# An RWKV mixer with a compact state, its token shift and masks partly on ScalarE, and another order of the trunk

## The chip, the cores and the metric

The kernel runs on one core of a Trainium2 chip. The core has a matrix engine (TensorE, PE in the profile, with its weight loads shown apart as PEld), VectorE (DVE), ScalarE (ACT), GpSimd (POOL) and SyncE (SP), which issues the transfers. TensorE writes to PSUM, eight banks of 128 partitions by 512 float32; the other data lie in SBUF. The metric is the device time of one execution in microseconds.

## The reference

Two layers over 256 tokens of width 1024. In each layer there is a SwiGLU feed-forward with a layer norm, a mixer whose output goes with a cross attention over 256 memory tokens through `w_out` into a second layer norm, and a second feed-forward with a third:

```python
x = layer_norm(ALPHA * x + 0.5 * swiglu(x, ffn1_w_gate[i], ffn1_w_up[i], ffn1_w_down[i]), ...)
proj = x @ w_in
heads = concat([mixer(proj[..., :k]), memory_attention(proj[..., k:], mem_k, mem_v)])
x = layer_norm(ALPHA * x + heads @ w_out[i], ...)
x = layer_norm(ALPHA * x + 0.5 * swiglu(x, ffn2_w_gate[i], ffn2_w_up[i], ffn2_w_down[i]), ...)
```

Layer 0 mixes by RWKV-7 with 12 heads of 64, layer 1 by stick-breaking attention. What the RWKV mixer computes:

```python
z = p + (prev - p) * mu                         # token shift, prev is the token before
kk = k * k_k; kk = kk * rsqrt(max(sum(kk * kk), 1e-24))
sa = state @ kk_t                               # for each token t, head by head, state 64x64
state = state * w_t - outer(sa, kk_t * a_t) + outer(v_t, k_t)
out_t = state @ r_t
```

and behind it a norm over each head, a bonus of r, k and v, and a gate.

## The kernel before, in words

**Tiling.** The 256 tokens are two halves of 128, each on the 128 partitions. A feed-forward of 2816 is cut into 11 blocks of 256 columns. For a block the gate and up weights come in four pieces of 128x1024 float32 and the down weights in two. `piece` splits each into a rounded part `hi` (a copy on ScalarE) and a rest `lo` (a subtraction on VectorE), and `mm3` makes one product out of three float32r matmuls (hi by hi, hi by lo, lo by hi). A block in the list `WHOLE` takes its down weights unsplit, as a plain float32 matmul, which the hardware does in two passes that the trace shows as two entries.

**Blocks for one half or for both.** A block is either *shared* (loaded once, used by both halves) or *solo* (loaded for one half alone, and again for the other). `LAGS` says how many blocks are solo. While a half is in its mixer, the other half's solo blocks are run beside it: `alternate` takes steps of the mixer and of the blocks in turns, by a table of weights (`RW` for RWKV, `SB` for the stick mixer), `HOLD` and `TAIL` say how many solo blocks are kept back for the time of `w_out` and for the end.

**The order.** Nothing is issued when it is written. `Plan` records every operation with its reads and writes, and a list scheduler with built-in durations puts them on the engines; it repeats this 24 times with shaken priorities from a fixed seed and keeps the shortest plan. The buffers (10 raw, 9 hi and 9 lo weight pieces; two PSUM banks for each of the tags `tp`, `gu`, `acc0`, `acc1`) are given out by the same plan. So each edit of the program or of a number can move instructions everywhere, and every instruction that is planned bears one line of the kernel (L606 before, L602 after, in `issue`); the names of the tiles tell them apart. A name ending in r with a number is a buffer, not a variable: `ps_2r` and `ps_3r` are the `tp` banks, `ps_26r` and `ps_27r` the `gu` banks, `ps_22r` to `ps_25r` the two `acc` pairs, and one buffer can hold several tiles in turn.

**The RWKV mixer** (`rwkv`) runs once per half, in two chunks of 64 tokens. `shifted` projects up to 512 columns, turns them (transposes into a `tp` bank), copies the turned part to SBUF, subtracts neighbouring tokens on VectorE and adds `mu` times the difference. Keys are normalised: two tensors (`qr[:, :, 0]` and `bt`) are each multiplied by the inverse norm. A triangular system of 64x64 per head and chunk is solved in blocks of 16, and doubled twice with masked copies of `L` (`_LEVELS`). Then the chunks follow one another: the state `S` takes 128 partitions (two heads of 64 in a pair) by 6 pairs by 2 by 64, with a pair's two 64x64 blocks on the diagonal of a 128x128 square and zeros off it. The output part from the state is

```python
nc.tensor.matmul(Ov[j // 3][cs, 2 * (j % 3):2 * (j % 3) + 2].rearrange("q h d -> q (h d)"), qr[:, j, 1, cs],
                 S[:, j].rearrange("p a d -> p (a d)"), start=False, stop=False)
```

and the state is updated in four parts of 64 rows, each by an addition from PSUM and a product with the decay.

**The gate of a feed-forward block** is either Tanh on ScalarE with two products on VectorE, or Silu with one. Before, `beside` chose by the stage: Tanh in the blocks beside a mixer, Silu elsewhere.

Of the kernel before, what the change touches and what calls it, by code (L numbers as in the profile page):

```python
# [21 lines left out]
P = 128  # L22
# [24 lines left out]
LAGS = ((5, 8), (4, 8))  # L47
FIRST = 2
PRE = (0, 0)
RW = dict(p0=0, p1=0, p2=0, p3=0, p4=0.5, lb=0, sub=14, rb=0.5, kq=1, nat=10, dy=4, dt=1.5, c0=1.0, c1=1, c2=6, c3=2, t0=0, t1=10)  # L50
SB = dict(z0=3.0, z1=0, ln=2.0, e0=1.0, e1=1.5, o=12)
HOLD = (2, 4)
TAIL = (2, 2)
# [5 lines left out]
BESIDE = (True, False)  # L59
WHOLE = (((0, 1, 2, 3, 4, 5, 6, 8, 9, 10), (0, 1, 2, 4, 5, 6, 7, 9)), ((3,), ()))  # L60
# [9 lines left out]
_LEVELS = [16, 32]  # L70


def _constants():
    i = np.arange(P)
    c, s = i // C, i % C
    t = np.arange(C)
    cols = {}
    cols["ident"] = np.eye(P)
    tri = np.zeros((P, 2, C + 1))
    for cc in range(2):  # L80
        tri[:, cc, :] = (c[:, None] == cc) & (s[:, None] <= np.arange(C + 1)[None, :] - 1)
    cols["tric"] = (-math.exp(-0.5) * tri).reshape(P, -1)
    mqr = np.stack([t[None, :] > s[:, None], t[None, :] >= s[:, None]], 1)
    cols["mqr"] = mqr.reshape(P, -1)
    lv = []
    for b in _LEVELS:
        lv.append((s[:, None] // (2 * b) == t[None, :] // (2 * b)) & (s[:, None] // b % 2 == 1) & (t[None, :] // b % 2 == 0))
    cols["lvl"] = np.stack(lv, 1).reshape(P, -1)
# [49 lines left out]
class Plan:  # L138
# [11 lines left out]
    @contextmanager  # L150
    def together(self):

        self.bundle = []
        yield
        o, self.bundle = self.bundle[0], None
        self.close(o)
# [453 lines left out]
def kernel(ctx, tc, const, x, mem, f1g, f1u, f1d, f2g, f2u, f2d, ln_g, ln_b, w_out, w_mem_kv,  # L610
# [22 lines left out]
    lvl = K_("lvl").rearrange("p (l t) -> p l t", t=C)  # L633
# [317 lines left out]
    def rwkv_constants():  # L951
# [6 lines left out]
        vc = cp.tile([P, 44], F32, tag="vc", name="vc")  # L958
        pt = ps("tp")
        nc.tensor.transpose(pt[:, :44], vrow, ident[:44, :44])  # L960
        nc.copy(vc, pt[:, :44])
        for n, a, b in (("mu", 0, 20), ("a0", 20, 26), ("k_k", 26, 32), ("k_a", 32, 38), ("r_k", 38, 44)):
# [3 lines left out]
        S = new(cp, [P, NT, 2, HD], F32, "S", "S")  # L966
# [5 lines left out]
    def rwkv(hf, res):  # L972
        ac = f"acc{hf}"
        mu, a0, k_k, k_a = R["mu"], R["a0"], R["k_k"], R["k_a"]
# [6 lines left out]
        def shifted(c0, n, dest):  # L981

            pn = project(hf, rw_in[0], c0, n)
            nt = min(n, SHIFT - c0) // P
            ch0 = c0 // P
            ptv = turned(pn, 0, n // P)
            pT = new(tp_, [P, 4, P + 1], F32, "tb", "pT", 2)
            came = nc.copy(pT[:, :nt, 1:], ptv[:, :nt])
            nc.vector.tensor_copy(pT[:, :nt, 0], lastc[:, ch0:ch0 + nt]).after.append(came.i)
            if hf < NHALF - 1:  # L990
                nc.vector.tensor_copy(lastc[:, ch0:ch0 + nt], pT[:, :nt, P])
            d = pn.rearrange("p (i t) -> p i t", t=P)
# [3 lines left out]
            if nt < n // P:  # L996
                mq = new(mp, [P, 2, P], F32, "mq", "mq")
                nc.copy(mq, ptv[:, nt:n // P], 0.125)
                return mq


        zl = sl("zl", [P, 2, P])
        mq = shifted(2304, 512, lambda i: zl[:, i])
# [46 lines left out]
        shifted(768, 512, lambda i: zk[:, i])  # L1050
        shifted(1280, 512, lambda i: zk[:, 4 + i] if i < 2 else zv[:, i - 2])
# [10 lines left out]
        nc.vector.tensor_mul(cv4(qr[:, :, 0]), cv4(bt), e1[:, :, :, 0:C])  # L1062
        nc.vector.tensor_mul(bt, bt, a)
# [20 lines left out]
        shifted(0, 512, lambda i: zr[:, i])  # L1084
        shifted(512, 256, lambda i: zr[:, 4 + i])
# [10 lines left out]
        shifted(1792, 512, lambda i: zv[:, 2 + i])  # L1096
# [125 lines left out]
        for l in range(len(_LEVELS)):  # L1222
            lastl = l == len(_LEVELS) - 1
            Lm, Y = hv(sl("Lm")), hv(sl("Y"))
            nc.vector.tensor_tensor(Lm, L, bc(lvl[:, l], 1, [P, NH, C]), ALU.mult)
# [49 lines left out]
        with nc.together():  # L1275
            for i in range(NH):
                for cs in both:
                    nc.tensor.matmul(Ov[i // 6][cs, i % 6], Sk[cs, i, 1], V[cs, i], start=i % 6 == 0, stop=False)
        yield "c0"
        for c, cs in enumerate(both):  # L1280
            first = hf == 0 and c == 0
            if not first:
                xs = six("tp")
                with nc.together():
                    for j in range(NT):
                        for p in range(2):
                            pr = slice(p * HD, (p + 1) * HD)
                            nc.tensor.matmul(xs[p][cs, j], qr[pr, j, 0, cs], S[pr, j, p], start=True, stop=True)
# [4 lines left out]
            with nc.together():  # L1293
                for i in range(NH):
                    nc.tensor.matmul(ub[i // 6][cs, i % 6], Tt[cs, i], X[cs, i], start=True, stop=True)
                    if c == 1:
                        nc.tensor.matmul(Ov[i // 6][both[0], i % 6], RB[both[0], i], U[both[0], i], start=False, stop=i % 6 == 5)
            nc.copy(U[cs, 0:6], ub[0][cs], -1.0)
            nc.copy(U[cs, 6:12], ub[1][cs], -1.0)
            if not first:  # L1300
                with nc.together():
                    for j in range(NT):
                        nc.tensor.matmul(Ov[j // 3][cs, 2 * (j % 3):2 * (j % 3) + 2].rearrange("q h d -> q (h d)"), qr[:, j, 1, cs],
                                         S[:, j].rearrange("p a d -> p (a d)"), start=False, stop=False)
            yield "c2"
            if not (hf == NHALF - 1 and c == 1):
                for g in range(2):
                    sb = ps("tp")
                    for a, b in ((kn, V), (bn, U)):
                        with nc.together():  # L1310
                            for i in range(6):
                                pr = slice(i % 2 * HD, (i % 2 + 1) * HD)
                                h = 6 * g + i
                                nc.tensor.matmul(sb[pr, i // 2 * HD:(i // 2 + 1) * HD], a[cs, h * HD:(h + 1) * HD], b[cs, h],
                                                 start=a is kn and i < 2, stop=a is bn and i >= 4)
                    for p in range(2):
                        pr = slice(p * HD, (p + 1) * HD)
                        st = S[pr, 3 * g:3 * g + 3, p]
                        nc.vector.tensor_tensor(st, st, sb[pr, :3 * HD].rearrange("q (i d) -> q i d", i=3), ALU.add)
                        nc.vector.tensor_tensor(st, st, bc(pc[pr, 3 * g:3 * g + 3, c], 2, [HD, 3, HD]), ALU.mult)  # L1320
                    yield "c3"
        with nc.together():
            for i in range(NH):
                nc.tensor.matmul(Ov[i // 6][both[1], i % 6], RB[both[1], i], U[both[1], i], start=False, stop=i % 6 == 5)
# [3 lines left out]
        for g in range(2):  # L1328
            gs = slice(6 * g, 6 * g + 6)
            nc.scalar.activation(sqo[:, gs], Ov[g], AF.Square)  # L1330
            nc.vector.tensor_tensor(o[:, gs], Ov[g], lg[:, gs], ALU.mult)
            nc.vector.tensor_reduce(hs[:, 0, gs], sqo[:, gs], AX.X, ALU.add)
# [147 lines left out]
    def blocks(w, seq, beside=False, whole=()):  # L1480
        waiting = []
        for c, halves in seq:
            hidden = yield from ffn_block(w, c, halves, beside, c in whole)
# [8 lines left out]
    for i in range(DEPTH):  # L1492
# [19 lines left out]
        run(blocks(w, solo(1, range(HEAD)), BESIDE[0], WHOLE[i][0]))  # L1512
        alternate(chain_steps(mixer(0, mixed)), blocks(w, solo(1, range(HEAD, lag1)), True, WHOLE[i][0]), steps)
# [11 lines left out]
        alternate(second, blocks(w, solo(0, range(lag2 - HOLD[i])), True, WHOLE[i][1]), steps)  # L1525
        run(chain_steps(mixed_out(1, mixed[1], w_out[i])), blocks(w, solo(0, range(lag2 - HOLD[i], lag2)), BESIDE[1], WHOLE[i][1]))
# [31 lines left out]
```

## Time and profile before

| | |
|---|---|
| median of the runs | 1084.11 us (1083.97 to 1085.16, 3 runs) |
| profiled execution | 1085.55 us, its span 1083.5 us |
| TensorE busy, matmul entries | 1063.7 us (98%), 6213 |
| VectorE busy, instructions | 890.6 us (82%), 1267 |
| ScalarE busy, instructions | 721.0 us (67%), 990 |
| bytes moved | 300.14 MB, mean 277 GB/s |
| granted TensorE clock | 0.997 of full |

A row of a window gives the stretch, its length, the busy time of PE, PEld, DVE, ACT and POOL with the count of instructions, then the granted clock, the mean share of the 16 DMA engines and GB/s. A row of a tile gives the operation, its count, the shortest, median and longest duration in ns, first and last start, and the shapes. A row of a timeline gives start, duration, operation, count. A wait gives who waited for whom, the sum in us, how often, and the longest. Ends of matmuls are modelled and overlap; the distance between two starts is what a matmul takes of the queue.

### The profile page before, as it was taken

To read this page: it belongs to the slowest core of one execution; us is meant where nothing else is said; L and a number is where in the kernel's file an instruction comes from. 1 tells how busy PE (TensorE), PEld (TensorE's weight loads), DVE (VectorE), ACT (ScalarE), POOL (GpSimd) and SP (SyncE) were. 2 spreads that over 40 slices of the span, in tenths; PEclk is the share of its full clock that TensorE was granted. 3 is DMA by queue.
4 is the path that set the end of the run, shared out by engine and by line. 5 is a ranking of instruction groups with operands and counts; after the bars stand their busy time and mean duration, and the time that the engine had idled before them with its cause. 6 is when DMAs were issued, how large, how long until landed. Compare 5 with 4: busy or idle time off the path is not lost.

```text
span 1083.5 us, 17483 instructions
## 1 busy us (share of the span) xinstructions
PE 1063.7 (98%) x6213; PEld 848.4 (78%) x6213; DVE 890.6 (82%) x1267; ACT 721.0 (67%) x990; POOL 2.7 (0%) x14
## 2 busy tenths in 40 slices
PE   7999999999999999999999999999999999999996
PEld 5888887867788777778888888888877787888885
DVE  6676679997999998787779965559889979987777
ACT  6565568765588774656658545547996999776652
POOL 0000000000000000000000000000000000000000
PEclk9999999999999999999999999999999999999998
DMA  9997869477797797699889976758978987999881
GB/s 312 335 355 243 261 211 363 134 256 250 216 317 262 237 312 259 221 344 317 261 264 353 335 252 197 225 182 274 372 275 283 389 310 236 394 368 304 258 284 58
DMA packets 210073, 300.14 MB, mean 277 GB/s; under 512 B 13716, under 2 KB 157248, under 8 KB 209986
## 3 DMA queue, kind: packets, MB, share of 16 engines
q1 hardware_dynamic: 209986, 299.03, 81.7%
q8 instruction: 48, 0.79, 0.3%
q14 instruction: 39, 0.32, 0.1%
HBM read 297.93 MB, written 1.05 MB: 276 GB/s over the span
## 4 chain that ended last, share of the span: by engine, by line
PE 94%; DVE 4%; DMA 1%; ACT 0%; issue 0%; SPq 0%; DVEq 0%; ACTq 0%
PE ps_27r L606 27%; PE ps_26r L606 27%; PE ps_25r L606 8%; PE ps_24r L606 8%; PE ps_22r L606 8%; PE ps_23r L606 8%; PE ps_3r L606 4%; PE ps_2r L606 4%; DMA raw_42r<-in_ffn_w_down_dram 1%; DVE x L606 1%; DMA raw_6r<-in_ffn_w_up_dram 0%; DVE Y_337r L606 0%; DVE xTl L606 0%; SPq L606 0%; DVE lo_5r L606 0%
## 5 line engine op out<-in xcount | busy, mean ns | idle before, releaser
L606 PE MATMUL ps_26r<-hi_4r,xTh 128*128 128x512 f32 x54 | 22.5, 416 | 2.8 <-ACT hi_4r L606 2.8
L606 ACT ACTIVATE h_32r<-ps_26r 128x256 f32<-128x256 f32 (+1 forms) x29 | 12.4, 426 | 18.9 <-PE ps_26r L606 18.9
L606 PE MATMUL ps_27r<-hi_19r,xTh 128*128 128x512 f32 x56 | 23.7, 423 | 0.0
L606 ACT ACTIVATE h_31r<-ps_27r 128x256 f32<-128x256 f32 (+1 forms) x32 | 13.5, 423 | 14.2 <-PE ps_27r L606 12.6
L606 PE MATMUL ps_27r<-hi_43r,xTh 128*128 128x512 f32 x54 | 22.2, 411 | 0.0
L606 PE MATMUL ps_26r<-lo_5r,xTh 128*128 128x512 f32 x54 | 21.7, 402 | 0.5 <-DVE lo_5r L606 0.5
L606 PE MATMUL ps_27r<-hi_7r,xTh 128*128 128x512 f32 x54 | 22.1, 410 | 0.0
L606 PE MATMUL ps_27r<-hi_16r,xTh 128*128 128x512 f32 x52 | 22.1, 425 | 0.0
L606 PE MATMUL ps_27r<-hi_19r,xTl 128*128 128x512 f32 x56 | 21.9, 391 | 0.0
L606 PE MATMUL ps_27r<-lo_20r,xTh 128*128 128x512 f32 x56 | 21.9, 391 | 0.0
L606 PE MATMUL ps_27r<-hi_4r,xTh 128*128 128x512 f32 x54 | 21.7, 402 | 0.0
L606 PE MATMUL ps_26r<-hi_4r,xTl 128*128 128x512 f32 x54 | 21.6, 400 | 0.0
L606 PE MATMUL ps_27r<-lo_44r,xTh 128*128 128x512 f32 x54 | 21.2, 393 | 0.2 <-DVE lo_44r L606 0.2
L606 PE MATMUL ps_26r<-hi_40r,xTh 128*128 128x512 f32 (+1 forms) x54 | 21.2, 393 | 0.0
L606 PE MATMUL ps_27r<-hi_43r,xTl 128*128 128x512 f32 x54 | 21.1, 392 | 0.0
L606 PE MATMUL ps_27r<-lo_8r,xTh 128*128 128x512 f32 x54 | 21.1, 391 | 0.0
L606 PE MATMUL ps_27r<-hi_7r,xTl 128*128 128x512 f32 x54 | 21.1, 391 | 0.0
L606 PE MATMUL ps_27r<-lo_5r,xTh 128*128 128x512 f32 x54 | 21.1, 391 | 0.0
L606 PE MATMUL ps_27r<-hi_4r,xTl 128*128 128x512 f32 x54 | 21.1, 390 | 0.0
L606 ACT ACTIVATE h_32r<-ps_27r 128x256 f32<-128x256 f32 (+1 forms) x25 | 10.6, 425 | 15.7 <-PE ps_27r L606 15.5
L606 PE MATMUL ps_26r<-hi_16r,xTh 128*128 128x512 f32 x52 | 21.0, 403 | 0.0
L606 PE MATMUL ps_26r<-hi_37r,xTh 128*128 128x512 f32 (+1 forms) x52 | 20.9, 402 | 0.0
(1918 smaller groups left out, 3951.5 us busy)
## 6 DMA issues: line engine op xcount, KB each, us to landing
raw_45r<-in_ffn_w_down_dram SPq DMA_DIRECT2D x18, 512.0 KB, 5.9
raw_18r<-in_ffn_w_gate_dram SPq DMA_DIRECT2D x33, 256.0 KB, 4.6
raw_18r<-in_ffn_w_up_dram SPq DMA_DIRECT2D x33, 256.0 KB, 3.0
raw_21r<-in_ffn_w_gate_dram SPq DMA_DIRECT2D x32, 256.0 KB, 4.3
raw_21r<-in_ffn_w_up_dram SPq DMA_DIRECT2D x32, 256.0 KB, 5.4
raw_15r<-in_ffn_w_down_dram SPq DMA_DIRECT2D x16, 512.0 KB, 5.3
raw_42r<-in_ffn_w_down_dram SPq DMA_DIRECT2D x15, 512.0 KB, 5.0
raw_15r<-in_ffn_w_gate_dram SPq DMA_DIRECT2D x29, 256.0 KB, 5.4
```

Of the source, the lines that this page charges most:

```text
L606: fn(*[at(x) for x in a], **{n: at(x) for n, x in k.items()})
```

## The change

- **State.** `S` loses its zero half: 128 partitions by 6 pairs by 64. The output part from the state is made head by head, with 64x64 matmuls like those of the product beside it; the output banks `Ov` hold the even and the odd heads instead of the lower and the upper six. The update of a chunk uses one PSUM bank and one addition and one product over all partitions. New orders between some of these steps are fixed by `after`.
- **Token shift.** The turned part isn't copied: ScalarE writes it times 1 - mu (`omm`), 128 columns at a time, and VectorE adds mu times the neighbour, read from PSUM. The last column of a group is kept by ScalarE or VectorE; for half 1 a small product `ml` and an addition bring in the column before.
- **Masks.** The masked copies of `L` are made by ScalarE with a mask on the partitions (`odd`, `quad`), on a tile that GpSimd clears.
- **Keys.** Only `bt` is multiplied by the inverse norm, and `qr[:, :, 0]` is made from it.
- **Gating.** `TANH` lists the blocks with Tanh, for each layer and feed-forward. Beside the mixer of half 1 in layer 0, block 4 becomes Silu, in layer 1 block 3.
- **Order.** `RW`, `SB`, `HOLD`, `TAIL`, `WHOLE` change; in layer 1's second feed-forward nine blocks are solo instead of eight.

The core of the diff:

```diff
-LAGS = ((5, 8), (4, 8))
+LAGS = ((5, 8), (4, 9))
-RW = dict(..., c0=1.0, c1=1, c2=6, c3=2, t0=0, t1=10)
-SB = dict(z0=3.0, z1=0, ln=2.0, e0=1.0, e1=1.5, o=12)
-HOLD = (2, 4)
-TAIL = (2, 2)
+RW = dict(..., c0=8, c1=3, c2=6, c3=2, t0=0, t1=1.5)
+SB = dict(z0=0, z1=0, ln=2.0, e0=1.0, e1=1.5, o=12)
+HOLD = (2, 3)
+TAIL = (3, 3)
-BESIDE = (True, False)
-WHOLE = (((0, 1, 2, 3, 4, 5, 6, 8, 9, 10), (0, 1, 2, 4, 5, 6, 7, 9)), ((3,), ()))
+TANH = (((0, 1, 2, 3, 4), (0, 1, 2, 3, 5, 9)), ((0, 1, 2, 3, 9), (0, 1, 2)))
+WHOLE = (((1, 2, 3, 4, 5, 6, 8, 9), (0, 1, 2, 4, 5, 6, 7, 9)), ((3,), ()))
...
-            came = nc.copy(pT[:, :nt, 1:], ptv[:, :nt])
-            nc.vector.tensor_copy(pT[:, :nt, 0], lastc[:, ch0:ch0 + nt]).after.append(came.i)
...
-            nc.vector.tensor_sub(d[:, :nt], pT[:, :nt, 0:P], pT[:, :nt, 1:])
-            for i in range(nt):
-                nc.vector.scalar_tensor_tensor(dest(i), d[:, i], mu[:, ch0 + i:ch0 + i + 1], pT[:, i, 1:], ALU.mult, ALU.add)
+                for q in range(m):
+                    nc.scalar.activation(dest[:, q], ptv[:, i + q], AF.Copy, scale=omm[:, ch + q:ch + q + 1])
+                    nc.vector.scalar_tensor_tensor(dest[:, q, 1:], ptv[:, i + q, :P - 1], mu[:, ch + q:ch + q + 1], dest[:, q, 1:], ALU.mult, ALU.add)
+                if hf > 0:
+                    nc.vector.tensor_tensor(dest[:, :, 0], dest[:, :, 0], ml[:, ch:ch + m], ALU.add)
...
-            for dst in (qr[:, :, 0, cs], bt[:, :, cs]):
-                nc.vector.tensor_mul(dst, dst, b_[c])
+            nc.vector.tensor_mul(bt[:, :, cs], bt[:, :, cs], b_[c])
+        nc.vector.tensor_mul(cv4(qr[:, :, 0]), cv4(bt), e1[:, :, :, 0:C])
...
-            nc.vector.tensor_tensor(Lm, L, bc(lvl[:, l], 1, [P, NH, C]), ALU.mult)
+                    nc.copy(Lm[:, :, ts], L[:, :, ts], K_("odd")[:, q:q + 1])
+                nc.copy(Lm[:, :, :2 * BLK], L[:, :, :2 * BLK], quad[:, 1:2])
...
+                    for j in range(NT):
+                        for p in range(2):
+                            pr = slice(p * HD, (p + 1) * HD)
+                            nc.tensor.matmul(Ov[p][cs, j], qr[pr, j, 1, cs], S[pr, j], start=j == 0 and c == 0, stop=False)
...
+                nc.vector.tensor_tensor(S, S, sb, ALU.add)
+                nc.vector.tensor_tensor(S, S, bc(pc[:, :, c], 2, [P, NT, HD]), ALU.mult)
```

What the plan makes of it, at three places. On TensorE, layer 0, half 0, between the first and the second chunk: `vn` by `kn` and `Lm` by `bn` are the state update, `S` by `qr` the products with the state, `hi` and `lo` the memory keys' projection beside them. Before, from the update to the product into the output banks `ps_22r` and `ps_23r`:

```order
L606 MATMUL ps_3r<-vn_307r,kn_306r 64x64 x6
L606 MATMUL ps_3r<-Lm_327r,bn_383r 64x64 x6
L606 MATMUL ps_2r<-vn_307r,kn_306r 64x64 x6
L606 MATMUL ps_2r<-Lm_327r,bn_383r 64x64 x6
L606 MATMUL ps_27r<-hi_43r,hi_7r 128x512
...
L606 MATMUL ps_3r<-S_110r,qr_376r 64x64
L606 MATMUL ps_2r<-S_110r,qr_376r 64x64
...
L606 MATMUL ps_22r<-S_110r,qr_376r 64x128 x3
L606 MATMUL ps_23r<-S_110r,qr_376r 64x128 x3
```

and after:

```order
L602 MATMUL ps_2r<-vn_311r,kn_310r 64x64 x12
L602 MATMUL ps_2r<-Lm_330r,bn_384r 64x64 x12
L602 MATMUL ps_25r<-raw_18r,hT_486r 128x512
L602 MATMUL ps_26r<-hi_43r,hi_13r 128x512
...
L602 MATMUL ps_23r<-S_110r,qr_377r 64x64
L602 MATMUL ps_22r<-S_110r,qr_377r 64x64
...
L602 MATMUL ps_3r<-S_110r,qr_377r 64x64
L602 MATMUL ps_2r<-S_110r,qr_377r 64x64
```

The update is one group in one bank, the product into the output banks comes first and in the same small form, and less other work stands between the update and the products that read the state.

On ScalarE, layer 0, half 0, in the projections of the mixer: `hi` is a weight split, `h` a copy of a projection, `pT` the turned part, `L` the shifted keys, `RB` and `g` the gates. Before:

```order
L606 ACTIVATE hi_16r<-raw_42r 128x1024
L606 ACTIVATE h_31r<-ps_26r 128x512
L606 ACTIVATE hi_43r<-raw_15r 128x1024
L606 ACTIVATE g_333r<-ps_22r 128x384
L606 ACTIVATE pT_324r<-ps_2r 128x4x128
L606 ACTIVATE g_333r<-ps_23r 128x384
```

and after:

```order
L602 ACTIVATE lastc<-ps_2r 128x4
L602 ACTIVATE RB_333r<-ps_23r,vc 128x128
L602 ACTIVATE L_345r<-ps_2r,vc 128x128
L602 ACTIVATE hi_19r<-raw_39r 128x1024
L602 ACTIVATE hi_16r<-raw_15r 128x1024
L602 ACTIVATE L_345r<-ps_2r,vc 128x128
L602 ACTIVATE hi_10r<-raw_42r 128x1024
L602 ACTIVATE h_31r<-ps_26r 128x512
L602 ACTIVATE g_336r<-ps_22r 128x384
L602 ACTIVATE L_345r<-ps_2r,vc 128x128
```

One copy out of the bank `ps_2r` has become four scaled ones with weight splits and other copies between them.

On SP, layer 1, half 1, the transfers of the stick mixer's projections (`sb_w_in`) and of the feed-forward blocks beside it. Before:

```order
L606 DMA raw_48r<-in_ffn_w_up_dram 128x2x256
L606 DMA raw_21r<-in_ffn_w_down_dram 128x1024
L606 DMA raw_15r<-in_ffn_w_down_dram 128x1024
L606 DMA raw_9r<-in_sb_w_in_dram 128x2x512
L606 DMA raw_12r<-in_sb_w_in_dram 128x2x512
```

and after:

```order
L602 DMA raw_15r<-in_sb_w_in_dram 128x2x512
L602 DMA raw_21r<-in_sb_w_in_dram 128x2x512
L602 DMA raw_42r<-in_sb_w_in_dram 128x2x512
L602 DMA raw_39r<-in_ffn_w_gate_dram 128x2x256
L602 DMA raw_39r<-in_ffn_w_up_dram 128x2x256
```

Before, the weights of three feed-forward blocks are fetched between the projections; after, all projections come first and nine solo blocks behind them.

More of the change, by code (lines that the diff above doesn't have):

```diff
@@ L69 @@
 BLK = 16
-_LEVELS = [16, 32]
 def _constants():
@@ L1274, in rwkv, with from_pairs @@
         nc.copy(X[:, 6:12], xb[1])
[L1275 to L1278, printed above, removed]
         yield "c0"
+        own = []
+        def from_pairs():
+            with nc.together() as made:
+                for i in range(NH):
+                    for c, cs in enumerate(both):
+                        nc.tensor.matmul(Ov[i % 2][cs, i // 2], Sk[cs, i, 1], V[cs, i], start=i < 2 and (hf == 0 or c == 1), stop=False)
+            own.extend(made)
+        if hf == 0:
+            from_pairs()
         for c, cs in enumerate(both):
             first = hf == 0 and c == 0
+            before = []
             if not first:
-                xs = six("tp")
-                with nc.together():
+                with nc.together() as before:
                     for j in range(NT):
@@ L1287, in rwkv @@
                             pr = slice(p * HD, (p + 1) * HD)
-                            nc.tensor.matmul(xs[p][cs, j], qr[pr, j, 0, cs], S[pr, j, p], start=True, stop=True)
+                            nc.tensor.matmul(Ov[p][cs, j], qr[pr, j, 1, cs], S[pr, j], start=j == 0 and c == 0, stop=False)
+                xs = six("tp")
+                with nc.together() as made:
+                    for j in range(NT):
+                        for p in range(2):
+                            pr = slice(p * HD, (p + 1) * HD)
+                            nc.tensor.matmul(xs[p][cs, j], qr[pr, j, 0, cs], S[pr, j], start=True, stop=True)
+                made[0].after.append(before[0].i)
                 for p in range(2):
@@ L1296, in rwkv @@
                     if c == 1:
-                        nc.tensor.matmul(Ov[i // 6][both[0], i % 6], RB[both[0], i], U[both[0], i], start=False, stop=i % 6 == 5)
+                        nc.tensor.matmul(Ov[i % 2][both[0], i // 2], RB[both[0], i], U[both[0], i], start=False, stop=i >= NH - 2)
+            solved = made[0].i
+            if hf > 0 and c == 0:
+                from_pairs()
+                own[0].after.append(solved)
             nc.copy(U[cs, 0:6], ub[0][cs], -1.0)
             nc.copy(U[cs, 6:12], ub[1][cs], -1.0)
[L1300 to L1304, printed above, removed]
@@ L1305, in rwkv @@
             yield "c2"
             if not (hf == NHALF - 1 and c == 1):
[L1307 to L1321, printed above, removed]
+                sb = ps("tp")[:, :MIX // 2].rearrange("q (j d) -> q j d", j=NT)
@@ new lines, in rwkv @@
+                for a, b in ((kn, V), (bn, U)):
+                    with nc.together() as made:
+                        for h in range(NH):
+                            pr = slice(h % 2 * HD, (h % 2 + 1) * HD)
+                            nc.tensor.matmul(sb[pr, h // 2], a[cs, h * HD:(h + 1) * HD], b[cs, h],
+                                             start=a is kn and h < 2, stop=a is bn and h >= NH - 2)
+                made[0].after.append(own[0].i)
+                nc.vector.tensor_tensor(S, S, sb, ALU.add)
@@ L1478, in spread, with blocks @@
         return [(c, h) for _, c, h in sorted(seq, key=lambda t: t[0])]
-    def blocks(w, seq, beside=False, whole=()):
+    def blocks(w, seq, beside=(), whole=()):
         waiting = []
         for c, halves in seq:
-            hidden = yield from ffn_block(w, c, halves, beside, c in whole)
+            hidden = yield from ffn_block(w, c, halves, c in beside, c in whole)
             yield from chain(*waiting)
@@ L1511 @@
         mixed = []
[L1512 to L1513 removed]
+        run(blocks(w, solo(1, range(HEAD)), TANH[i][0], WHOLE[i][0]))
+        alternate(chain_steps(mixer(0, mixed)), blocks(w, solo(1, range(HEAD, lag1)), TANH[i][0], WHOLE[i][0]), steps)
         norm(1, 2.0 * ALPHA, 4.0 * LN_EPS, gb)
```

95 lines of the change are left out of this document (51 added, 44 removed).

## The prediction

> **What bounds the kernel now.** I read the page first (busy shares and the chain that ended last), then the stretches of 100 us, then TensorE's own waits, and last the timeline of TensorE inside the mixer.
>
> ```profile
> PE 1063.7 (98%) x6213; PEld 848.4 (78%) x6213; DVE 890.6 (82%) x1267; ACT 721.0 (67%) x990; POOL 2.7 (0%) x14
> PE 94%; DVE 4%; DMA 1%; ACT 0%; issue 0%; SPq 0%; DVEq 0%; ACTq 0%
> 0.00:100.00 100.00, 92.31 (x409) 75.07 (x410) 66.48 (x72) 60.05 (x75) 1.62 (x9) 1.00 0.93 318
> 200.00:300.00 100.00, 97.58 (x1089) 74.21 (x1089) 92.32 (x178) 59.85 (x106) 0.84 (x4) 1.00 0.68 220
> 300.00:400.00 100.00, 100.00 (x671) 77.70 (x668) 98.16 (x177) 77.78 (x125) 0.20 (x1) 1.00 0.82 279
> 900.00:1000.00 100.00, 100.00 (x483) 81.38 (x482) 90.93 (x111) 75.94 (x95) 0.00 (x0) 1.00 0.98 342
> 1040.00:1083.50 43.50, 34.59 (x156) 27.94 (x154) 33.59 (x59) 17.81 (x24) 0.00 (x0) 0.94 0.40 135
> PE ps_2r L606 <- DMA x<-in_x_dram: 4.4, 1, 4.4
> PE ps_26r L606 <- ACT hi_4r L606: 2.8, 1, 2.8
> PE ps_2r L606 <- DVE xTl L606: 1.1, 1, 1.1
> 306.81 5.44 PE ps_27r L606 x24
> ```
>
> TensorE carries 94% of the chain that ended last. Of its 19.8 us of idle time 7.7 lie in the first 100 us (the first input 4.4, the first weight piece 2.8) and 8.9 behind the last matmul; only 2.4 us lie in 200 to 300 and less than 1 us anywhere else. The last row is the unit of the sum: 24 float32r matmuls of 128x512 in a row take 5.44 us, 227 ns each. VectorE is the second engine: 92 and 98% busy through the RWKV mixer. So a term that shortens TensorE's own queue shortens the run; VectorE or ScalarE work counts only where it becomes a wait.
>
> The Trainium skill, "Perfetto Trace Analysis", section Identifying the Most-Contended Engine, holds that matmul busy time is a bad measure and weight-load time the better one; by it the 78% of PEld would leave room below 98%, and a change that feeds TensorE sooner would be worth more than I say. The row of 24 speaks against much room: inside it nothing waits.
>
> **The change on TensorE.** The wide products on the state and the 64x64 products beside them, in the second chunk of half 0, and one detour to 64x64 form:
>
> ```profile
> 267.84 0.40 PE L606 MATMUL ps_26r<-hi_43r,lo_8r 128*128 128x512 f32 x1
> 268.16 0.56 PE L606 MATMUL ps_3r<-vn_307r,kn_306r 64*64 64x64 f32 x12
> 269.26 0.52 PE L606 MATMUL ps_2r<-Lm_327r,bn_383r 64*64 64x64 f32 x12
> 269.71 0.50 PE L606 MATMUL ps_27r<-hi_43r,hi_7r 128*128 128x512 f32 x1
> 270.04 0.39 PE L606 MATMUL ps_27r<-lo_44r,hi_7r 128*128 128x512 f32 x1
> ...
> 272.08 0.22 PE L606 MATMUL ps_3r<-S_110r,qr_376r 64*64 64x64 f32 x1
> ...
> 272.66 0.22 PE L606 MATMUL ps_3r<-S_110r,qr_376r 64*64 64x64 f32 x1
> ...
> 272.82 0.87 PE L606 MATMUL ps_22r<-S_110r,qr_376r 128*64 128x128 f32 x6
> 273.52 0.82 PE L606 MATMUL ps_23r<-S_110r,qr_376r 128*64 128x128 f32 x6
> 274.27 0.27 PE L606 MATMUL ps_3r<-L_342r,Tt_326r 64*64 64x64 f32 x1
> ...
> 228.83 1.02 PE L606 MATMUL ps_24r<-raw_12r,pT_324r 128*128 128x512 f32 x2
> 229.70 0.38 PE L606 MATMUL ps_3r<-cst,Lm_327r 128*128 128x128 f32 x2
> ```
>
> *State product.* The six 128x64-form matmuls (each two passes) on the block-diagonal state run from 272.82 to 274.27, 1.45 us. They become twelve 64x64 matmuls (24 passes) on the compact state, in the form of the product just before, where from 272.08 to 272.66 ten pairs of passes, on two row halves at once, take 0.58 us: 12 pairs take 0.70. There are three such places (the first chunk has no state): 3 x (0.70 - 1.45) = **-2.25 us**. Were the pairs not to overlap, 24 x 0.058 = 1.39 us would leave -0.2; that is the other end.
>
> *Changes of tile form.* Going to 64x64 form costs 0.32 instead of 0.23 before it (267.84 to 268.16), the last group 0.45 instead of 0.35 (269.26 to 269.71; the twelve-row groups start 0.35 apart inside) and the first matmul after it 0.33 instead of 0.23: 0.29 us for the way there and back. Counted over the two orders, the form changes 100 times before and 90 times after, 8 of the 10 beside the wide products. Ten at 0.145 are 1.45; four of them sat between two small forms and showed only some 0.07, and 0.15 is in the term above already: **-1.0 us**, ends -0.5 and -1.45.
>
> *One block less in whole float32* (block 0 of half 1): four float32 matmuls at 0.87 us (228.83 to 229.70, x2 passes) are 3.48; the twelve float32r ones that replace them are 12 x 0.227 = 2.72: **-0.75 us**. The other dropped entry of that list (10) was never used.
>
> The number of transposes, projections, solves and state-update products is the same; the update is issued as one group instead of two at no change of passes. TensorE's sum is **-4.0 us**, with ends -1.5 and -4.5.
>
> **The change beside TensorE.**
>
> ```profile
> L606 DVE TENSOR_TENSOR S_110r<-S_110r,pc_340r x12: 341/352/355, 270.0 to 429.6; 64x192 f32<-64x192 f32 x12
> L606 DVE TENSOR_TENSOR L_342r<-L_342r,ps_3r x3: 538/557/557, 273.3 to 432.1; 64x384 f32<-64x384 f32 x3
> L606 DVE TENSOR_TENSOR Lm_327r<-Lm_327r,ps_22r x1: 550/550/550, 208.7 to 208.7; 128x384 f32<-128x384 f32 x1
> L606 DVE TENSOR_TENSOR h_31r<-pT_324r x6: 417/422/691, 173.0 to 346.9; 128x256 f32<-128x256 f32 x4, 128x512 f32<-128x512 f32 x2
> L606 DVE COPY pT_324r<-lastc x6: 161/165/168, 171.8 to 346.5; 128x2 f32<-128x2 f32 x4, 128x4 f32<-128x4 f32 x2
> L606 DVE TENSOR_TENSOR Lm_327r<-L_342r,cst x4: 949/950/951, 240.0 to 405.9; 128x768 f32<-128x768 f32 x4
> L606 ACT ACTIVATE pT_324r<-ps_2r x11: 382/387/601, 172.0 to 372.3; 128x256 f32<-128x256 f32 x7, 128x512 f32<-128x512 f32 x4
> L606 ACT ACTIVATE RB_330r<-ps_22r,vc x3: 359/367/368, 184.4 to 184.9; 128x128 f32<-128x128 f32 x3
> L606 ACT ACTIVATE RB_330r<-ps_25r,vc x3: 404/414/422, 332.6 to 333.1; 128x128 f32<-128x128 f32 x3
> L606 ACT ACTIVATE T_336r<-Tt_326r,cst x8: 630/643/648, 238.2 to 399.5; 128x192 f32<-128x192 f32 x8
> L606 ACT ACTIVATE hi_19r<-raw_6r x9: 1039/1052/1062, 81.6 to 1025.2; 128x1024 fp32r<-128x1024 f32 x9
> L606 DVE TENSOR_TENSOR lo_20r<-raw_6r,hi_19r x9: 1209/1226/1226, 82.7 to 1026.3; 128x1024 fp32r<-128x1024 f32 x9
> 172.00:202.00 30.00, 30.00 (x163) 24.68 (x162) 26.94 (x49) 26.54 (x43) 0.20 (x1) 1.00 0.81 286
> 322.00:352.00 30.00, 30.00 (x211) 24.89 (x210) 29.88 (x60) 26.30 (x44) 0.00 (x0) 1.00 0.78 274
> 1010.00:1074.00 64.00, 64.00 (x290) 52.43 (x289) 49.14 (x66) 35.81 (x46) 0.00 (x0) 1.00 0.67 222
> ```
>
> VectorE loses 24 half-height state operations (8.4 us) for 6 of 128x384 (3.3): -5.1; four products with the key norm at 0.55: -2.2; four masks at 0.95: -3.8; and in the token shift, per half, the subtractions (four of 0.69, two of 0.42) and six boundary copies of 0.165, with six more for half 0 and seven small additions for half 1: -9.1 in all. Sum -20 us. ScalarE gains 20 scaled copies a half at 0.39 (between the two RB rows, the same shape from PSUM with a pointer) for six plain ones (3.2): +9.2 in both halves, small boundary copies some +1.4, masks +3.6 (0.64 or less each). The weights of block 0 and of one more feed-forward block loaded for each half apart (eight pieces) give VectorE 8 x 1.22 and ScalarE 8 x 1.06 back, and 3.1 MB and ten issues on SP's queue. Choosing Silu for a few blocks takes one 0.4 us VectorE product from each; the larger memsets go to idle POOL. I cost all this at nothing: TensorE shows no idle time in these stretches, and the cover is the feed-forward block run beside the mixer. Without that cover the price is that of the rivals.
>
> What is queued behind the longer steps: on ScalarE the weight splits (1.05 us each) stand between the scaled copies, and a PSUM bank of the transposes ("tp", two in all) is now held until VectorE has read it four times, where one copy of 0.6 us used to free it. TensorE's next transposes wait for that bank. Waits can also shrink: the small ones between matmuls in the mixer, the 2.4 us of idle time, and what the modelled ends hide, for which I allow as much again. I take 0 for the balance, ends -4 and +3.
>
> **Sum.** The profiled execution took 1085.55 us, 2.05 of it outside its span of 1083.5; minus 4.0 that is 1081.5. It lies 1.4 above the median of the runs, so from the median 1084.11 I come to **1080.1 us** (-0.37%). About 0.2% (2.2 us) is what a measurement of this kernel can tell from no change.
>
> **Rivals.** *VectorE's relief is worth more* (chance 0.15): waits in the mixer go as well, -4 more: 1076. For it speaks VectorE's 98% in 300 to 400; against it that TensorE has no idle time there.
>
> *ScalarE takes the gain back* (0.20). Between 172 and 202 it is busy 26.5 us of 30, and again 26.3 between 322 and 352. About twelve scaled copies for three plain ones fall in each stretch: +3.1, so 29.6 and 29.4, full. If the held banks then stop TensorE by 1 to 2 us in each, 1082 to 1084 results, say 1083: no change. Against it: the same copies are interleaved with projections that keep TensorE fed for 5.4 us each. The Trainium skill, "ScalarE: Activation LUTs", section Rules for kernel authors, would leave multiplications to VectorE; followed, the shift would stay where it was, and moving it is what this rival charges for.
>
> *Slower: the transfers at the end* (0.15). DMA has a share of 0.98 at 342 GB/s between 900 and 1000. A feed-forward block loaded for one half alone is 3.1 MB for 36 matmuls, 8.2 us, so 380 GB/s, and now nine run for half 0 and five close together at the end of half 1. With prefetching exhausted the added 3.1 MB cost 9.2 us at 342 GB/s: 1089. It decides once over 6 us of these show. Against it: from 1010 to 1074 the rate is only 222 GB/s, room for 7.7 MB.
>
> **Chances.** Forecast 0.50 (own range 1078.5 to 1081.9), more relief 0.15, gain taken back 0.20, transfers 0.15. Faster: 0.50 + 0.15 less 0.01 for the edge = 0.64; same 0.21; slower 0.15. The range from 1076.5 (TensorE's -4 with nearly all waits gone) to 1086.0 (TensorE's low end -1.5 and +3 of waits, a little beyond) leaves the transfers' 0.15 above it and some 0.05 below.
>
> **What would show it.** The three products of qr with S at about 0.7 us in 64*64 form, right beside the product into ps_2r and ps_3r; four fewer two-pass raw matmuls; state operations on VectorE six times at 0.55; ScalarE near full around 172 to 202, with TensorE still free of idle time. Wrong it would be if PE idle time appears there with an ACT or DVE releaser, if PE waits for lo or hi pieces behind DMA after 840, or if the 64x64 pairs on the two row halves do not overlap.

## The result, and the profile after

The changed kernel takes 1075.26 us (1073.62 to 1075.61, 4 runs) against 1084.63 for the kernel before beside it (1083.97 to 1085.25, 4 runs): a ratio of 0.9911, 95% interval 0.9893 to 0.9928, 9.4 us less. The profiled execution took 1075.53 us, its span 1073.7. The forecast was 1080.1 with a range of 1076.5 to 1086.0: the sign was right, the gain more than twice as large as said, and the time lies 1.2 us below the range.

The busy times and the chain's shares on the page of the kernel after, and its stretches (length, PE, PEld, DVE, ACT, POOL, clock, DMA share, GB/s):

```profile
PE 1055.9 (98%) x6253; PEld 848.2 (79%) x6253; DVE 880.6 (82%) x1227; ACT 730.2 (68%) x1037; POOL 4.3 (0%) x18
PE 94%; DVE 4%; DMA 1%; ACT 1%; issue 0%; SPq 0%; DVEq 0%; ACTq 0%
0.00:100.00 100.00, 92.96 (x407) 75.67 (x408) 66.56 (x73) 59.92 (x75) 1.30 (x9) 1.00 0.97 317
172.00:202.00 30.00, 30.00 (x165) 25.01 (x164) 26.12 (x40) 28.47 (x57) 0.21 (x1) 1.00 0.90 306
200.00:300.00 100.00, 99.29 (x1118) 76.92 (x1117) 90.22 (x168) 66.46 (x123) 1.84 (x6) 1.00 0.74 239
300.00:400.00 100.00, 100.00 (x706) 77.99 (x705) 93.59 (x166) 82.47 (x146) 1.21 (x3) 1.00 0.85 281
900.00:1000.00 100.00, 100.00 (x455) 82.41 (x454) 91.45 (x107) 73.27 (x88) 0.00 (x0) 1.00 1.04 353
```

```profile
PE ps_26r L602 <- ACT xTh L602: 1.2, 1, 1.2
PE ps_2r L602 <- ACT memKT L602: 0.6, 1, 0.6
```

TensorE still sets the end. Of the 9.8 us that the span lost, 7.8 are TensorE's busy time (1063.7 to 1055.9) and 2.0 its idle time (19.8 to 17.8). In the first 100 us, where the loads are waited for, 0.7 of idle time went, and 1.7 in 200 to 300; 0.5 came back in 800 to 900, where a wait of 1.2 at 819 (second fence, from the list of TensorE's waits) replaces one of 0.5. The 0.7 need not be the change's: in the other executions of these two orders the first two waits add up to between 5.7 and 7.2 us. ScalarE is nearly full from 172 to 202, as expected, and TensorE has no idle time there; at 900 to 1000 the transfers run at 353 GB/s, and TensorE waits for none.

The chain in order of time (start, length, what) shows the 1.7 us, behind the first RWKV half, where its output `Y` is finished and turned for `w_out`. Before:

```profile
286.80 1.50 DVE Y_337r L606 x4
288.30 0.29 issue
288.59 0.55 DVE Y_337r L606
289.14 1.14 DVE lo_8r L606
290.27 0.60 DVE xTl L606
290.87 1.13 DVE lo_20r L606
292.00 0.60 DVE xTl L606
```

and after:

```profile
283.36 1.15 DVE lo_8r L602
...
285.53 0.43 ACT memKT L602
...
286.00 0.66 PE ps_2r L602 x4
286.65 0.45 PE ps_3r L602 x4
...
288.62 3.44 PE ps_23r L602 x15
```

Before, VectorE holds the chain from 286 to 293 while TensorE waits 1.1 us for `xTl` and again for less. After, `Y` is finished at 283.4 instead of 289.1, while TensorE's wait for `memKT` just ahead of it ends at 286.0 instead of 289.3; from there the chain is TensorE's.

The product of `qr` with `S` into the output banks, in the timeline of TensorE (start, duration, operation), second chunk of half 0:

```profile
267.20 0.27 PE L602 MATMUL ps_23r<-S_110r,qr_377r 64*64 64x64 f32 x1
...
267.90 0.22 PE L602 MATMUL ps_22r<-S_110r,qr_377r 64*64 64x64 f32 x1
267.95 0.22 PE L602 MATMUL ps_3r<-S_110r,qr_377r 64*64 64x64 f32 x1
```

Its 24 passes take 0.75 us, right beside the product into `ps_3r` and `ps_2r`. So it is in the second chunk of half 1; in the first chunk of half 1 the two stand apart, and it takes 0.80. On VectorE the state operations are now whole-height (busy us, mean ns, idle before them):

```profile
L602 DVE TENSOR_TENSOR S_110r<-S_110r,pc_343r 128x384 f32<-128x384 f32 x3 | 1.7, 555 | 0.1
```

### The profile page after: what moved, and what is told of

The parts are those of the page before. It is cut to its first block, busy times and chain, and to the rows that moved or that the text cites. A ratio compares the mean times of both kernels' runs of the same rounds, so it can differ in the third digit from the quotient of the medians.

```text
span 1073.7 us, 17563 instructions
## 1 busy us (share of the span) xinstructions
PE 1055.9 (98%) x6253; PEld 848.2 (79%) x6253; DVE 880.6 (82%) x1227; ACT 730.2 (68%) x1037; POOL 4.3 (0%) x18
## 4 chain that ended last, share of the span: by engine, by line
PE 94%; DVE 4%; DMA 1%; ACT 1%; issue 0%; SPq 0%; DVEq 0%; ACTq 0%
PE ps_26r L602 29%; PE ps_27r L602 28%; PE ps_24r L602 8%; PE ps_25r L602 8%; PE ps_22r L602 7%; PE ps_23r L602 7%; PE ps_2r L602 4%; PE ps_3r L602 4%; DVE x L602 1%; DMA raw_12r<-in_sb_w_in_dram 1%; DMA raw_6r<-in_ffn_w_up_dram 0%; DVE lo_5r L602 0%; DVE st_564r L602 0%; DVE Y_340r L602 0%; DVE lo_44r L602 0%
## 5 line engine op out<-in xcount | busy, mean ns | idle before, releaser
L602 PE MATMUL ps_26r<-hi_4r,xTh 128*128 128x512 f32 (+1 forms) x66 | 27.0, 409 | 1.9 <-ACT hi_4r L602 1.9
L602 PE MATMUL ps_26r<-lo_5r,xTh 128*128 128x512 f32 (+1 forms) x66 | 26.0, 394 | 0.5 <-DVE lo_5r L602 0.5
L602 PE MATMUL ps_26r<-hi_4r,xTl 128*128 128x512 f32 (+1 forms) x66 | 25.9, 392 | 0.0
L602 PE MATMUL ps_26r<-hi_13r,xTh 128*128 128x512 f32 x50 | 21.0, 419 | 1.2 <-ACT xTh L602 1.2
L602 PE MATMUL ps_26r<-hi_19r,xTh 128*128 128x512 f32 (+1 forms) x54 | 22.0, 407 | 0.0
L602 PE MATMUL ps_26r<-hi_7r,xTh 128*128 128x512 f32 x52 | 21.7, 417 | 0.0
L602 PE MATMUL ps_27r<-hi_13r,xTh 128*128 128x512 f32 x52 | 21.6, 415 | 0.0
L602 PE MATMUL ps_27r<-hi_16r,xTl 128*128 128x512 f32 x54 | 21.2, 392 | 0.0
L602 PE MATMUL ps_27r<-lo_17r,xTh 128*128 128x512 f32 x54 | 21.1, 390 | 0.0
L602 PE MATMUL ps_26r<-hi_7r,xTl 128*128 128x512 f32 x52 | 20.8, 400 | 0.0
```

The lines of the kernel that those rows point to most:

```text
L602: fn(*[at(x) for x in a], **{n: at(x) for n, x in k.items()})
```

## The experiments

Three explanations were at hand. *Steps*: the products on the state, the form changes and block 0, as the prediction had them. *Addresses* (A): between the two traces the float32r products from the second `hT` buffer had changed their pace, and that buffer had moved, because the slot that it shares with `pT`, the turned part with one more token (4 x 129 columns), shrank from 2112 to 2048 bytes when `pT` went. *Order* (W): this one plan avoids waits that another plan of the same code would have.

**Addresses.** In these kernels all instructions stand in the same order on every engine as in the kernel they come from; only the size of a slot differs, by a constant added to one line of `slot`.

```diff
-        self.size[key] = max(..., self.size.get(key, 0))
+        self.size[key] = max(..., self.size.get(key, 0), 528 * (tag == "tb"))   # after_one_off
+        self.size[key] = max(..., self.size.get(key, 0), 32 * (tag == "pc"))    # after_both_off
+        self.size[key] = max(..., self.size.get(key, 0), 544 * (tag == "tb"))   # before_both_on
+        self.size[key] = max(..., self.size.get(key, 0), 576 * (tag == "tb"))   # before_256
```

> The kernel after with the slot of the transposed hidden tile (hT, two buffers) padded from 2048 to 2112 bytes; the instructions and their order on every engine stay the same, only addresses move: the second hT buffer now starts 64 bytes off a multiple of 128 relative to the weight pieces that are multiplied with it, as it did in the kernel before. Theory A (addresses set the pace of the float32r products): its 456 products of 128x512 take 233.5 ns each instead of 227.2, +2.8 us, so about 1078.1; the first buffer's stay at 227.2. Theory B (the gain came from order and waits, the pace in the two traces differed by chance or by its neighbours): no change, 1075.3, and both buffers at 227.

> The kernel after with a small tile ahead of hT padded by 64 bytes, so that both hT buffers stand 64 bytes off a multiple of 128 relative to the weight pieces; same instructions, same order. Theory A: all 912 products at 233.5 ns, +5.7 us, about 1081. A form of A in which an absolute address counts (multiples of 128 good for hT, as its first buffer had in the kernel before): no change or a small gain. Theory B: no change, 1075.3.

> The kernel before with the slot of hT padded from 2112 to 2176 bytes, so that both buffers are multiples of 128 bytes away from the weight pieces; same instructions, same order. Theory A: the 444 products from the second buffer fall from 233.5 to 227.4 ns, -2.7 us, about 1081.9. Theory B: 1084.6, no change.

> The kernel before with the slot of hT padded from 2112 to 2304 bytes; same instructions, same order. 128 bytes off was as slow as 64 in the padding to 2176 (233 ns), so the rule is put again: an hT buffer is fast where it stands a multiple of 256 bytes from the weight pieces. Theory A by that rule: both buffers at 227.5 ns, -2.8 us, about 1082.4 against 1085.2. Theory B (a second buffer of this kernel is slow wherever it stands): no change, 1085.2.

| kernel | `hT` buffers off a multiple of 256 bytes from the weights | mean distance of two starts, ns | time, ratio to before (95%) |
|---|---|---|---|
| after | 0, 0 | 227.2, 227.1 | 1075.26, 0.9911 (0.9893 to 0.9928) |
| after_one_off | 0, 64 | 227.6, 233.3 | 1077.82, 0.9936 (0.9922 to 0.9949) |
| after_both_off | 64, 64 | 233.4, 233.4 | 1081.43, 0.9965 (0.9953 to 0.9978) |
| before | 0, 64 | 227.5, 233.5 | 1084.63, 1 |
| before_both_on | 0, 128 | 227.8, 233.0 | 1085.44, 1.0002 (0.9993 to 1.0011) |
| before_256 | 0, 0 | 227.5, 227.3 | 1081.96, 0.9971 (0.9959 to 0.9982) |

Where a tile stands is read off the program's memory map; the distances in time are means over the products that have others of their kind on both sides. A time's ratio is to runs of the kernel before beside it, whose medians go from 1084.63 to 1085.24, so times of different rows compare to about half a us. The pace can be read in the chain too, where six `hT` products in a row (into `ps_22r` to `ps_25r`) take 1.36 us or 1.40. After:

```profile
503.03 1.36 PE ps_25r L602 x6
543.30 1.36 PE ps_23r L602 x6
```

after_one_off, the same two places:

```profile
503.43 1.36 PE ps_25r L602 x6
543.90 1.40 PE ps_23r L602 x6
```

after_both_off:

```profile
503.46 1.40 PE ps_25r L602 x6
544.17 1.40 PE ps_23r L602 x6
```

The kernel before, the first from the second buffer, the other from the first:

```profile
495.68 1.40 PE ps_24r L606 x6
504.20 1.36 PE ps_24r L606 x6
```

and the same places in before_256:

```profile
494.94 1.36 PE ps_24r L606 x6
503.35 1.36 PE ps_24r L606 x6
```

Theory A holds: one buffer is worth 2.6 us, both 6.2, and before_256 gains 2.9 from a change of addresses alone. before_both_on was a miss that mended the rule: 128 bytes off is nearly as slow as 64. Theory B falls, since the pace follows the address with the same instructions in the same order.

Two more asked whether it is the distance or the address itself, and whether `xT`, the stationary tile of the other 2784 such products, obeys too.

```diff
-    xTt = [xp.tile([P, KT, SEQ], F32R, tag=n, name=n) for n in ("xTh", "xTl")]
+    xTt = [xp.tile([P, q + KT * SEQ], ...)[:, q:]... for n, q in (("xTh", LINE), ("xTl", 0))]   # after_xt_off, and 64 * (tag == "pc")
-        vc = cp.tile([P, 64], F32, tag="vc", name="vc")
+        vc = cp.tile([P, 80], F32, tag="vc", name="vc")                                          # after_all_shift
```

> The kernel after with the turned input xT (both halves of its split) moved 64 bytes off a multiple of 256 relative to the weight pieces, hT kept aligned; same instructions, same order. Theory A (the distance between the stationary tile and the moving one counts, whatever the tile): the xT products, some 2750 of 128x512, take 6 ns more each, +15 to +17 us, about 1091, hT's stay at 227. Theory A2 (only the feed-forward's hT is touched, for instance by its writers): no change, 1075.3.

> The kernel after with every tile behind the constants moved by 64 bytes together; same instructions, same order. Theory A (only the distance counts): no change, 1075.3, all float32r products at 227 to 228 ns. If the absolute address counts: up to 5.7 us from hT alone, 1081, or more from xT.

With `xT` off the time was 1088.78 us (ratio 1.0034, 1.0022 to 1.0046), slower than the kernel before; with everything moved together 1074.34 (0.9900, 0.9886 to 0.9915). Rows of the chain of after_xt_off, 24 `xT` products and six of `hT`:

```profile
463.56 5.60 PE ps_27r L602 x24
506.94 1.36 PE ps_25r L602 x6
```

and the first of these in after_all_shift:

```profile
460.00 5.47 PE ps_27r L602 x24
```

So the distance counts, for both tiles. The rise of 13.5 us is below the 15 to 17 expected, in part because `xT`'s products went from 228.2 ns, not 227, to 233.3: 2784 x 5.1 ns = 14.2.

**The compact state alone, and all but the compact state.** The first is the kernel before with the lines of the change on the state (the diff shown with the change), the second the kernel after without them.

> The kernel before with the compact state alone (64x64 products on the state, the update in one group, two state operations instead of eight); shift, masks, key norm, numbers of the order and addresses of hT as before. By the prediction's steps: state product -2.25, eight form changes less -0.8, together -3.0, about 1082.2. Rival, the gain needs the rest of the change (a wait takes its place): 1085.2. More than -4: the eased VectorE pays on TensorE too.

> The kernel after with the wide block-diagonal state put back (128x64 products, four updates); all else as after, hT aligned. By the prediction's steps +3.0, about 1078.3. If the compact state is worth nothing by itself: 1075.3. If the new numbers of the order fit only the new code: over 1079.5.

before_compact took 1083.69 us (0.9985, 0.9976 to 0.9994), 1.2 less where 3.0 was expected. The time of the matmuls in 128x64 and 64x64 form, from start to start, fell from 59.0 to 56.0 us; 0.6 of the 59.0 is a pause at 224 us that before_256 and before_both_on, in the same order, don't have (58.4). So 2.4 to 3.0 are there. But the plan's new order gave a part of it back: TensorE changes form 96 times, not the 92 that eight fewer would make, and of the waits in its list (who for whom, us, times, longest) the first stands where the kernel before has one of 1.1 us and the other two are new:

```profile
PE ps_2r L606 <- DVE xTl L606: 1.0, 1, 1.0
PE ps_3r L606 <- DVE xTl L606: 1.0, 1, 1.0
PE ps_24r L606 <- DVE Y_337r L606: 0.5, 1, 0.5
```

after_wide took 1084.47 (0.9995, 0.9986 to 1.0004), 9.2 more where 3.0 was expected: the two forms took 2.6 us more, form changes rose from 90 to 100, and the rest is the order, with one wait that cost twice. The timeline of TensorE in after_wide (start, duration, operation, idle time before and its cause), and below it the granted clock of that stretch (the number before the last two):

```profile
293.59 0.45 PE L602 MATMUL ps_3r<-cst,Y_340r 128*128 128x128 f32 x2 [1.68 <-DVE xTl L602]
293.79 0.68 PE L602 MATMUL ps_23r<-hi_19r,xTh 128*128 128x512 f32 x1
295.38 0.63 PE L602 MATMUL ps_23r<-hi_19r,xTh 128*128 128x512 f32 x1
295.81 0.63 PE L602 MATMUL ps_23r<-lo_20r,xTh 128*128 128x512 f32 x1
297.66 0.39 PE L602 MATMUL ps_23r<-hi_16r,xTh 128*128 128x512 f32 x1
```

```profile
290.00:292.00 2.00, 1.92 (x16) 1.21 (x12) 2.00 (x4) 2.00 (x4) 0.00 (x0) 1.00 0.54 206
294.00:298.00 4.00, 4.00 (x12) 2.77 (x11) 4.00 (x8) 3.77 (x11) 0.00 (x0) 0.59 0.45 129
293.89:297.30 3.41, 3.41 (x10) 2.32 (x9) 3.41 (x7) 3.18 (x12) 0.00 (x0) 0.50 0.38 138
```

After the wait for `xTl` the clock falls to one half for 3.41 us (the last row; 0.59 is a mean with full speed at its end), and the float32r products there stand 0.43 us apart instead of 0.23.

**The order.** Five kernels ask what the plan is worth. In two, the numbers that pace it are exchanged between the kernels; these also set how many blocks are solo and, in after_old_numbers, which take Tanh. In three only the seed of its random shakes differs.

```diff
-LAGS = ((5, 8), (4, 9))            # after_old_numbers: LAGS, RW, SB, HOLD, TAIL, TANH
+LAGS = ((5, 8), (4, 8))            #   as in the kernel before; before_new_numbers the reverse, without TANH
-SEED = 8617
+SEED = 1                           # after_seed, before_seed; 2 in after_seed2
```

> The kernel after with the numbers that pace the order (lags, steps of the mixers, held and tail blocks, blocks with Tanh) as in the kernel before; compact state, shift, masks, the key norm and the float32r block 0 stay. If the new numbers carry the part of the gain that neither the state product, the form changes, block 0 nor the addresses explain (some 2.5 us of smaller waits): 1077 to 1079. If the gain lies in the rewritten parts alone and the order is only a fit to them: within 1 us of 1075.3.

> The kernel before with the numbers that pace the order (lags, steps, held and tail blocks) as in the kernel after. Put back into the kernel after, the old numbers cost 4.3 us, most of it waits. If the new numbers are better for any of the two codes: about 1081. If they only fit the code that they were set for: 1084 to 1088, with waits in other places.

> The kernel after with another seed for the planner's random shakes (1 for 8617): the same operations, addresses of hT aligned, only the order differs. Theory W (some 3 to 4 us of the gain are waits that this one order avoids, and any new order of this code brings them back): 1077 to 1080, with waits of TensorE over 0.5 us at new places. Rival (the waits left are set by the code, the order matters little): within 1 us of 1075.3.

> As the run before with seed 2. Theory W: 1077 to 1080 again, at other places. Rival: within 1 us of 1075.3.

> The kernel before with seed 1: the same operations in another order, second hT buffer off as before. Theory W: the order of before is one that was fitted too, so 1086 to 1089. Rival: within 1 us of 1084.9.

| kernel | time, us | ratio to before (95%) | TensorE busy, rest of the span |
|---|---|---|---|
| after | 1075.26 | 0.9911 (0.9893 to 0.9928) | 1055.9, 17.8 |
| after_old_numbers | 1079.60 | 0.9950 (0.9937 to 0.9962) | 1057.6, 20.2 |
| after_seed | 1080.89 | 0.9966 (0.9951 to 0.9981) | 1057.9, 21.1 |
| after_seed2 | 1080.88 | 0.9962 (0.9947 to 0.9977) | 1058.3, 20.2 |
| before | 1084.63 | 1 | 1063.7, 19.8 |
| before_seed | 1083.55 | 0.9991 (0.9981 to 1.0000) | 1064.9, 19.3 |
| before_new_numbers | 1088.36 | 1.0027 (1.0017 to 1.0038) | 1065.1, 21.2 |

Busy time and rest are those of the profiled execution; that of before_seed took 1086.10 us, the longest of its ten, and has a fall of the clock (last section), so its two numbers are not those of the median.

Three other plans of the code after cost 4.3 to 5.6 us more, half of it idle time, half TensorE's busy time with more form changes (94 to 96, not 90). With both seeds the wait for `xTl` behind the first mixer half, gone in the kernel after, is back (1.0 and 1.3 us); with the old numbers that one stays away, and others of 1.2, 0.7 and 0.6 us stand elsewhere. TensorE's waits in after_seed, beyond the first loads:

```profile
PE ps_3r L602 <- DVE h_31r L602: 1.3, 1, 1.3
PE ps_2r L602 <- DVE xTl L602: 1.0, 1, 1.0
PE ps_2r L602 <- DVE x L602: 0.7, 1, 0.7
PE ps_26r L602 <- ACT memKT L602: 0.6, 1, 0.6
```

The new numbers aren't better in themselves: in the old code they cost 3.5 us, with two waits of 2.0 and 2.2 us, each followed by a fall of the clock. Theory W holds for the code after, and the price is above its ranges: 1080.9 with both seeds where 1077 to 1080 was said, 1079.6 with the old numbers where 1077 to 1079 was. For the code before it missed: another seed cost nothing there, it was rather 1 us faster. As far as one other seed can tell, the order of before was an ordinary one of its code; the order of after is 4 to 6 us better than the three others tried.

**Block 0 in whole float32 again.**

```diff
-WHOLE = (((1, 2, 3, 4, 5, 6, 8, 9), ...
+WHOLE = (((0, 1, 2, 3, 4, 5, 6, 8, 9), ...
```

> The kernel after with feed-forward block 0 of half 1 in the first layer put back to whole float32 in its down projection. By the prediction's step +0.75 of TensorE work, 1076.0. By theory W the planner's new order adds waits as well: 1077 to 1080; the products' own time is then read from the trace (four of 0.87 us against twelve of 0.227).

It took 1083.30 us (0.9983, 0.9973 to 0.9992), 8.0 more, even above W's range. TensorE is busy 1059.3 us (+3.4) and 21.6 idle (+3.8), changes form 100 times, and has the wait for `xTl` behind the first mixer half again (1.2 us). Since the plan moved, the price of the block in the run's time, 0.75 by the prediction, can't be read from it. The products' own time can: a two-pass product takes 0.86 us there (429 ns from entry to entry), so four of them take 3.4 us against 2.7 for twelve of 0.227. (A pass is here an entry of the trace; how the hardware goes about a float32 product, the trace does not show.)

## Why the prediction was wrong

**A term was missing: addresses.** The step that failed first is "I cost all this at nothing", under *The change beside TensorE*: the copy `pT` was costed as VectorE and ScalarE time, but its width of 129 columns also set the slot that `hT` shares. Without it both buffers stand at a good distance, and TensorE's own products get faster: -2.6 us by after_one_off, -2.9 by before_256. With that term alone the forecast would have been 1077.5. What is left of the gain beyond that is idle time (2.0) and TensorE's time (1.1), the next two paragraphs.

**"I take 0 for the balance" of the waits, ends -4 and +3.** The idle time fell by 2.0, inside the ends. It fell in the place that VectorE held, behind the mixer's first half, which the rival *VectorE's relief is worth more* named only for 300 to 400. The row of that wait (1.1 us for `xTl`) was shown in the prediction and not followed along the chain, where VectorE stands for 7 us around it. It is not VectorE's lighter load by itself that ended the wait: with both other seeds the same code has it again.

**State product, -2.25.** Right: 0.75 us in two places and 0.80 in the third where 0.70 was said (1.45 before), so -2.1; the pairs overlap. *Changes of tile form, -1.0*: 100 to 90 as counted; together with the state product the two small forms fell from 59.0 to 55.6 us, -3.4, or -2.8 without the pause at 224 us, against -3.25 said. *Block 0, -0.75*: the four two-pass products are gone, worth 0.7 by their own pace; their price in a fixed order stays untested. Compared at equal addresses (after_one_off) TensorE's busy time fell by 5.1 where -4.0 was said; the 1.1 beyond weren't traced to one place.

**What the sum hid.** The terms are right as TensorE work and still not what the change would have given in any order: the compact state alone returned 1.2 of 3.0, and the code after in three other orders stands 4 to 6 us below the kernel before, 2.6 to 2.9 of them addresses. That the whole arrived, and more, is the new plan. The prediction has no term for the order of the plan, neither a price nor a spread: that the sum's -4.0 came in full was luck with this one order.

**The rivals.** *VectorE's relief is worth more* comes nearest with its 1076, and not for its reason: TensorE had no idle time in 300 to 400, before or after, and its idle time fell by 2.0 in all, not 4. *ScalarE takes the gain back* fell: 28.5 us busy of 30 between 172 and 202, close to the 29.6 worked out, and no wait of TensorE. *The transfers at the end* fell: 353 GB/s and no wait. The Trainium skill, "Perfetto Trace Analysis", section Identifying the Most-Contended Engine, holds weight-load time a better measure of how near TensorE is to its limit than matmul time. Here weight loads stayed at 848 us in both kernels while the time fell by 9.4, so that measure did not follow the gain; how much room TensorE still has, no run here shows.

## What to carry to other kernels

When an edit removes or resizes a tile, look at where the tiles behind it land before counting instructions: here one slot that became 64 bytes shorter was worth about as much as the compact state's products. Where a planner sets the order, price an edit against several orders of the same code; a single before and after compares two plans as much as two codes. And follow a wait along the chain to the engine that holds it, even if it is only 1 us.

## What the runs showed of the hardware

**Distance of the two operands.** A float32r matmul of 128x512 takes 227 ns if its stationary tile starts a multiple of 256 bytes from its moving tile, and 233 if it is 64 or 128 bytes off (192 wasn't tried), up to 13.5 us of this kernel. The plain float32 products don't show it: they take 429 ns from entry to entry in the kernel after and in after_both_off, where their `hT` is 64 bytes off. Why, the runs don't show. The Trainium skill, "SBUF — State Buffer", section SBUF: two separate sides, says that at its SBUF ports TensorE never waits on another engine. That is about other engines; these runs show that the distance of TensorE's own two operands can cost 6 ns a product.

**The clock after short waits.** Waits of 1.7 us (after_wide), 2.0 and 2.2 us (before_new_numbers) were each followed by 3.41 us at half the clock, in which a product took 0.43 us instead of 0.23; half of 3.41, some 1.7 us, is an estimate of what each fall cost. The length of one wait does not decide. The wait of 1.2 us in the kernel after was not followed by a fall, but the profiled execution of before_seed has one behind two waits of 0.6 us and shorter gaps, here as two windows, ahead of it and in it:

```profile
287.46:290.87 3.41, 2.08 (x15) 1.36 (x16) 3.41 (x6) 2.80 (x7) 0.00 (x0) 1.00 0.54 160
290.87:294.28 3.41, 3.41 (x14) 2.39 (x11) 3.29 (x7) 2.62 (x8) 0.00 (x0) 0.50 0.55 154
```

In the 3.41 us ahead of these four falls TensorE was idle for 1.3 to 2.2 us in all; where the border lies, the runs don't show. The Trainium skill, "TensorE: Matmul & The Clock Gate", section What's actually happening, puts the fall after at least one idle window of about 3.4 us; here a stretch of that length sufficed in which TensorE was idle for less than two thirds.
